# Gate product of the second block in seven block products instead of eight, with the block sums of its weights formed by transfers in DRAM

## The chip, the cores and the metric

One core of a Trainium2 chip runs the whole program in one launch. The metric is device time in microseconds (us). The kernel before took 2392.82 us (median of three runs, 2391.46 to 2393.68).

## The reference, cut to what matters

Two transformer-like blocks run one after the other on 512 tokens of width 2048, in fp32. The change touches only the end of the second block:

```python
def second_block(x, p, ...):
    ...
        merged = g_a * (o_a @ w_up_a[l]) + g_b * (o_b @ w_up_b[l])
        x = x + merged @ w_out[l]
        x = x + jax.nn.sigmoid(x @ w_ple_gate[l]) * (p[l] @ w_ple[l])
    return rms_norm_2(x, final_g)
```

The *gate product* is `x @ w_ple_gate`, a 512 x 2048 by 2048 x 2048 product. Each result passes a sigmoid, is multiplied by `p @ w_ple` (formed at the start of the kernel and kept in DRAM as `ple`), is added to `x`, and at last each token's row is normalised by its mean square and multiplied by `final_g`.

## The kernel before

**Precision.** TensorE multiplies fp32r tiles, which hold a rounded fp32. So each fp32 operand is split (`split`, L331) into a high part `hi`, a rounded copy made on ScalarE (`whi<-wraw`), and a low part `lo = raw - hi`, made on VectorE (`wlo<-wraw,whi`). `mm3` (L339) then issues three matmuls: hi by hi, hi by lo, lo by hi. Where the weight streams (as in the gate product), the first of the three needs the weight's `hi`, and the second its `lo`.

**Units.** All weight products are a list `spine` of `Unit`s (L237). A unit is one weight block: a DMA on SP's queue into a 4 KB-per-partition buffer (512 KB in all, `wraw`), its split into two more such buffers, and its matmuls. There are ten of these buffers (`NW`). A second pool of 78 buffers of 2 KB per partition (`NSLOT`) holds activations.

**Order.** The program is written out by hand in one order, and each engine and each queue runs its share in that order. While the matmuls of unit i are written, `ahead` (L148) writes DMAs up to unit i+3 (`LD = 4`) and splits up to unit i+2 (`LS = 3`) and no further, provided that a small time model (`Clock`, L147) does not have VectorE or ScalarE over 5 us ahead of TensorE. Unit i+3's split is thus written after everything that belongs to unit i. Side work (generators in `Sides`, L181) is put between matmuls by `pump`, one step at a time, as long as the model has VectorE and ScalarE at most 3 us ahead of TensorE.

**The last stages.** `w_in_2` (units 127 to 302 of the list), then `w_up_a_2`/`w_up_b_2` (32 units), then the `w_out_2` product (L2031, 32 units, *out2* below). Out2 makes the new x in 16 tiles of 128 channels x 512 tokens; each (L2012) is added, split into `x2h`, `x2l`, transposed by TensorE (`px2`) and stored to DRAM token by token (`x2t`).

**The gate product.** Five column groups (`GATES`: 512, 512, 512, 256, 256). The 128 x 128 tiles of x2 are the stationary operand, the weight streams. In the groups of 512, `panel_units` (L852) makes 8 units; a unit covers two of the 16 channel tiles and, for each of four token blocks b, issues 2 x 3 matmuls of 512 columns, 24 in all. In the unit that ends a group, each b's sum is followed by `after_gate` (L2065): tanh on ScalarE, two VectorE operations (`tgate<-tgate,plel` and `x<-tgate,x`), a square with row sum on ScalarE, and a VectorE product with `final_g`. The last group (`whole_units`, L878) holds all its weight and finishes token block after token block; `finish` (L2090) forms 1/sqrt on VectorE in small steps (`part`), scales the four column blocks on ScalarE and VectorE, and stores them.

Of the kernel before, what the change touches and what calls it, by code (L numbers as in the profile page):

```python
# [8 lines left out]
F32 = mybir.dt.float32  # L9
# [72 lines left out]
GATES = ((0, 512), (512, 512), (1024, 512), (1536, 256), (1792, 256))  # L82


def blocks():
# [4 lines left out]
    def cut(ks, c0, c1, n):  # L90
# [9 lines left out]
    gate = [b for i, (c0, n) in enumerate(GATES)  # L100
            for b in cut(rows(KT, (512 if i == len(GATES) - 1 else 1024) // n), c0, c0 + n, n)]
# [135 lines left out]
class Unit:  # L237
    def __init__(self, src, shape, mm, pre=None, hold=1, half=False):

        self.src, self.shape, self.mm, self.pre, self.hold, self.half = src, shape, mm, pre, hold, half  # L240
        self.raw = self.hi = self.lo = None


def emit(ctx, tc, I, out):
# [1171 lines left out]
    done = {"oa": [], "ob": [], "sg": []}  # L1416
# [579 lines left out]
    x2h, x2l = [None] * KT, [None] * KT  # L1996
    x2_d = dram("x2t", (128, TB, D))
    xl = {}

    def load_x1(m):  # L2000
        if m < KT:
            xl[m] = slot([128, 512], "x1l")
            dma("G", xl[m], x1_d[m])

    def out2_pre(m):
        def fn():
            if m == 0:
                load_x1(0)
            load_x1(m + 1)
        return fn  # L2010

    def after_o2(m):  # L2012
        def fn(ps):
            x = xl.pop(m)
            tt(x, ps, x, OP.add)
            x2h[m], x2l[m] = slot([128, 512], f"x2h{m}", F32R), slot([128, 512], f"x2l{m}", F32R)
            split(x, x2h[m], x2l[m])
            sides.spawn(x2_gen(m, x))
        return fn

    def x2_gen(m, x):
# [7 lines left out]
        dma("G", x2_d[:, :, m * 128:(m + 1) * 128], o)  # L2029

    for m in range(KT):  # L2031
        spine += ch_units("w_out_2", m * 128, 128, after_o2(m), out2_pre(m), KT, (mgh, mgl))


    ssq = cp.tile([128, TB, 8], F32, name="ssq")
    x3 = {}
    pl_ = {}

    def gate_load(i):
        if i >= len(GATES):  # L2040
            return
        c0, n = GATES[i]
        for b in range(TB):
            if c0 % 512 == 0:
                x3[b, c0 // 512] = slot([128, 512], "x3")
            p = slot([128, n], "plel")
            dma("G", p, ple_d[b][c0 // 512][:, c0 % 512:c0 % 512 + n])
            dma("G", x3[b, c0 // 512][:, c0 % 512:c0 % 512 + n], x2_d[:, b, c0:c0 + n])
            pl_[i, b] = p

    def gate_pre(i):
        def fn():
            if i == 0:
                sides.drain()
# [7 lines left out]
    last = len(GATES) - 1  # L2062
    part = {}

    def after_gate(i):  # L2065
        def fn(b, ps):
            c0, n = GATES[i]
            t = slot([128, n], "tgate")
            act(t, ps[:, :n], AF.Tanh, scale=0.5)
            x = x3[b, c0 // 512][:, c0 % 512:c0 % 512 + n]  # L2070
            fg = pl_["fg", c0 // 512][:, c0 % 512:c0 % 512 + n]
            stt(t, t, 1.0, pl_[i, b], OP.add, OP.mult)
            stt(x, t, 0.5, x, OP.mult, OP.add)
            if i < last:
                act(t, x, AF.Square, accum_out=ssq[:, b, i:i + 1])
                tt(x, x, fg, OP.mult)
                if i == last - 1:
                    sides.spawn(part_gen(b))
                return
            stt(t, x, 1.0, x, OP.mult, OP.mult, accum_out=ssq[:, b, i:i + 1])  # L2080
            sides.spawn(finish(b, x, fg))
        return fn
# [136 lines left out]
```

## Time and profile before

| | |
|---|---|
| median of three runs | 2392.82 us |
| the profiled execution | 2393.15 us, its span 2391.4 us |
| TensorE busy | 99% of the span |
| VectorE, ScalarE, GpSimd busy | 62%, 39%, 11% |
| mean DMA rate | 141 GB/s |

The profile names PE for TensorE's matmuls, PEld for its weight loads, DVE for VectorE, ACT for ScalarE, POOL for GpSimd and SP for SyncE, whose queue loads the weights. Times of the timeline are us from the start of the span. A matmul's row has its own duration, longer than the distance between starts since matmuls overlap. "[0.78 <-DVE x1l L283]" means that the engine stood idle for 0.78 us before the row and that the end of that VectorE operation released it.

### The profile page before, as it was taken

The page shows a single profiled execution, that of the slowest core. Times are in us where ns is not written, and L with a number is a line of the kernel's source. Part 1 is how long each engine was busy: PE and PEld are TensorE (multiplying, and loading weights), DVE is VectorE, ACT ScalarE, POOL GpSimd, SP SyncE. Part 2 cuts the span into 40 slices and gives each one's busy share as a digit, 9 for nine tenths or more (in the row PEclk, how much of TensorE's full clock was granted, in tenths as well). Part 3 has the DMA queues.
Part 4 walks back from the last instruction along what each step waited for, and adds up shares of the span by engine and source line. Part 5 has one row for each costly group of instructions (what it writes and reads, how often), then busy time and mean ns, then how long its engine had stood idle before and what let it go on. Part 6 is the DMA issues. An engine that isn't in the chain of part 4 may idle for free.

```text
span 2391.4 us, 31046 instructions
## 1 busy us (share of the span) xinstructions
PE 2360.1 (99%) x11587; PEld 1985.0 (83%) x11587; DVE 1478.4 (62%) x2816; ACT 929.6 (39%) x1724; POOL 251.1 (11%) x376
## 2 busy tenths in 40 slices
PE   7999999999999999999999999999999999999998
PEld 5778889888888988888888888888888888888887
DVE  6787988788865367558878437777233444333336
ACT  5423265655533343335444234544233222222223
POOL 0000030332212001000000000000012100111201
PEclk9999999999999999999999999999999999999999
DMA  9986732333355333222222232222345533444633
GB/s 334 351 272 241 257 129 71 124 124 101 111 181 175 92 108 132 90 92 89 93 86 96 93 97 89 93 85 89 124 164 175 202 105 109 140 141 145 219 103 118
DMA packets 115783, 336.98 MB, mean 141 GB/s; under 512 B 15326, under 2 KB 15620, under 8 KB 115632
## 3 DMA queue, kind: packets, MB, share of 16 engines
q1 hardware_dynamic: 92016, 260.83, 32.8%
q0 software_dynamic: 22752, 73.02, 9.1%
q8 instruction: 91, 1.49, 0.3%
q10 hardware_dynamic: 864, 1.14, 0.1%
q14 instruction: 60, 0.49, 0.1%
HBM read 297.18 MB, written 37.75 MB: 140 GB/s over the span
## 4 chain that ended last, share of the span: by engine, by line
PE 85%; issue 6%; DVE 5%; ACT 2%; DMA 1%; POOL 1%; SPq 0%; POOLq 0%; DVEq 0%; ACTq 0%
PE pch L320 45%; PE ppan L320 14%; PE pp L320 9%; PE po L320 6%; PE psc L320 3%; PE pO L320 3%; PE pPT L324 2%; PE pearly L320 1%; DVE wlo L283 1%; PE pple L320 1%; PE pmod L534 1%; ACT whi L314 0%; DVE cA L283 0%; PE pada L320 0%; DMA wraw<-in_w_in_dram 0%
## 5 line engine op out<-in xcount | busy, mean ns | idle before, releaser
L283 DVE TENSOR_TENSOR wlo<-wraw,whi 128x1024 fp32r<-128x1024 f32 (+5 forms) x401 | 468.0, 1169 | 210.1 <-ACT whi L314 204.9
L314 ACT ACTIVATE whi<-wraw 128x1024 fp32r<-128x1024 f32 (+5 forms) x403 | 399.4, 1003 | 326.1 <-PE pch L320 115.1
L320 PE MATMUL pch<-h2h,whi 128*128 128x512 f32 x1216 | 483.3, 397 | 0.0
L320 PE MATMUL pch<-h2h,wlo 128*128 128x512 f32 x1216 | 474.9, 391 | 0.0
L320 PE MATMUL pch<-h2l,whi 128*128 128x512 f32 x1216 | 474.6, 390 | 0.0
L320 PEld LDWEIGHTS pch<-h2h,wlo 128*128 128x128 f32 x1216 | 228.2, 188 | 48.6
L320 PEld LDWEIGHTS pch<-h2h,whi 128*128 128x128 f32 x1216 | 228.6, 188 | 41.1
L320 PEld LDWEIGHTS pch<-h2l,whi 128*128 128x128 f32 x1216 | 228.8, 188 | 40.8
L314 ACT ACTIVATE P<-psc,sm 128x512 f32<-128x512 f32 (+3 forms) x160 | 83.6, 526 | 134.1 <-DVE sm L306 103.9
L320 PE MATMUL pp<-hh,whi 128*128 128x512 f32 x320 | 126.0, 394 | 0.2 <-DVE acc L283 0.2
L320 PE MATMUL pp<-hh,wlo 128*128 128x512 f32 x320 | 124.7, 390 | 0.0
L320 PE MATMUL pp<-hl,whi 128*128 128x512 f32 x320 | 124.6, 389 | 0.0
L320 PE MATMUL ppan<-whi,x2h 128*128 128x512 f32 (+1 forms) x320 | 111.0, 347 | 0.0
L320 PE MATMUL ppan<-whi,x2l 128*128 128x512 f32 (+1 forms) x320 | 110.9, 347 | 0.0
L320 PE MATMUL ppan<-wlo,x2h 128*128 128x512 f32 (+1 forms) x320 | 110.9, 347 | 0.0
L320 PE MATMUL pch<-mgh,whi 128*128 128x512 f32 x256 | 101.1, 395 | 0.0
L320 PE MATMUL pch<-mgh,wlo 128*128 128x512 f32 x256 | 99.9, 390 | 0.0
L320 PE MATMUL pch<-mgl,whi 128*128 128x512 f32 x256 | 99.7, 389 | 0.0
L320 PE MATMUL pch<-oh,whi 128*128 128x512 f32 x256 | 99.6, 389 | 0.0
L320 PE MATMUL pch<-ol,whi 128*128 128x512 f32 x256 | 99.6, 389 | 0.0
L320 PE MATMUL pch<-oh,wlo 128*128 128x512 f32 x256 | 99.6, 389 | 0.0
L314 ACT ACTIVATE PTh<-pPT 128x512 fp32r<-128x512 f32 (+1 forms) x120 | 59.5, 528 | 91.1 <-PE pPT L324 88.7
(500 smaller groups left out, 4635.0 us busy)
## 6 DMA issues: line engine op xcount, KB each, us to landing
wraw<-in_w_in_dram SPq DMA_DIRECT2D x199, 512.0 KB, 3.5
wada<-in_w_mod_dram SPq DMA_DIRECT2D x128, 256.0 KB, 5.4
wraw<-in_w_out_dram SPq DMA_DIRECT2D x64, 512.0 KB, 3.5
wgate<-in_w_gate_dram SPq DMA_DIRECT2D x64, 256.0 KB, 4.9
wraw<-in_w_ple_gate_dram SPq DMA_DIRECT2D x28, 512.0 KB, 3.5
sg<-mg POOLq DMA_DIRECT2D x32, 256.0 KB, 2.5
wraw<-in_w_up_b_dram SPq DMA_DIRECT2D x16, 512.0 KB, 3.5
sgl<-sg POOLq DMA_DIRECT2D x32, 256.0 KB, 6.1
```

The source lines that it names most:

```text
L283: V.tensor_tensor(o, a, b, op=op)
L314: A.activation(o, a, fn, **k)
L320: T.matmul(o, l, r, start=start, stop=stop_)
L324: T.transpose(o, a, i)
L534: T.matmul(acc[32 * q:32 * q + 32, :], cc[:, k, :], w.rearrange("p s n -> p (s n)"), start=first, stop=last_)
```

## The change

The gate product is done in two pairs of 512-wide column blocks (p = 0, 1). Within a pair x is cut in four quarters (rows: tokens 0 to 255 and 256 to 511; columns: channels 0 to 1023 and 1024 to 2047) and the weight in four (1024 x 512 each). Seven products of a quarter-sized left form with a quarter-sized right form (Strassen's method in Winograd's version) take the place of eight. They run in the order 1, 7, 6, 2, 5, 3, 4.

- Left forms: `F[q, k]`, one 128 x 2 x 256 tile (hi and lo) for each product q and each of 8 channel tiles, 56 tiles. Those of products 1, 7, 6 are made beside out2 (`early_forms`), the others beside the first products of pair 0 (`late_forms`). Both pairs use them.
- Right forms: three products use blocks of the weight as they are; for the other four, sums of blocks are formed in DRAM by 64 POOL transfers of 512 KB, half of them copies and half accumulating (`wsums`), one after every second unit from unit 150 on.
- A unit is now two channel tiles by two token blocks j: 12 matmuls of 512 columns. A product has 4 units and a pair 28. `after_prod`, called for each j in a product's fourth unit, puts the products together; products 2, 5, 3 and 4 each complete a result and go through `gated` (tanh, two VectorE operations, square).
- The product with `final_g` is moved: for pair 0 into the start of products 7, 6 and 2 of pair 1, for pair 1 behind `gated`.
- The very last product holds its four units' weight and runs j = 0 whole and j = 1 in two halves of 256 columns; `finish` is called per token block as before.
- Out2's 16 tiles come in the order 0, 8, 1, 9, ... instead of 0, 1, 2, ...; x2h and x2l of whole tiles are no longer made.
- `thin`, a way to form a unit's low part by an accumulating DMA, is in the code but off (`THIN = False`): all low parts that were on VectorE stay there.

```diff
-GATES = ((0, 512), (512, 512), (1024, 512), (1536, 256), (1792, 256))
+THIN = False
+SUMS = 150
...
-    gate = [b for i, (c0, n) in enumerate(GATES)
-            for b in cut(rows(KT, (512 if i == len(GATES) - 1 else 1024) // n), c0, c0 + n, n)]
+    gate = cut(rows(KT, 2), 0, D, 512)
...
+    O2 = [m for k in range(8) for m in (k, k + 8)]
...
     def after_o2(m):
         def fn(ps):
-            x = xl.pop(m)
+            x = x2r[m] = xl.pop(m)
             tt(x, ps, x, OP.add)
-            x2h[m], x2l[m] = slot([128, 512], f"x2h{m}", F32R), slot([128, 512], f"x2l{m}", F32R)
-            split(x, x2h[m], x2l[m])
             sides.spawn(x2_gen(m, x))
+            if m >= 8:
+                sides.spawn(early_forms(m - 8))
...
+    def quarters(k):
+        a, c = x2r[k], x2r[k + 8]
+        return a[:, 0:256], c[:, 0:256], a[:, 256:512], c[:, 256:512]
+    def form(q, k, x):
+        t = slot([128, 2, 256], "F" + q, F32R)
+        act(t[:, 0], x, AF.Copy)
+        yield [t]
+        tt(t[:, 1], x, f(t[:, 0]), OP.subtract)
+        F[q, k] = t
+    def early_forms(k):
+        x11, _, x21, x22 = quarters(k)
+        yield [x22]
+        yield from form("1", k, x11)
+        s = slot([128, 2, 256], "fs")
+        tt(s[:, 0], x11, x21, OP.subtract)
+        tt(s[:, 1], s[:, 0], x22, OP.add)
+        yield [s]
+        yield from form("7", k, s[:, 0])
+        yield from form("6", k, s[:, 1])
+    def late_forms():
+        for k in range(8):
+            yield
+            yield from form("2", k, quarters(k)[1])
+        for k in range(8):
+            x11, x12, x21, x22 = quarters(k)
+            yield
+            s = slot([128, 2, 256], "fs")
+            tt(s[:, 0], x21, x22, OP.subtract)
+            yield [s]
+            yield from form("5", k, s[:, 0])
+            tt(s[:, 1], x12, x11, OP.subtract)
+            tt(s[:, 1], s[:, 1], s[:, 0], OP.add)
+            yield [s]
+            yield from form("3", k, s[:, 1])
+            x2r.pop(k)
+        for k in range(8):
+            yield
+            yield from form("4", k, x2r[k + 8][:, 256:512])
+            x2r.pop(k + 8)
...
+    PROD = ("1", "7", "6", "2", "5", "3", "4")
+    PAIRS = (0, 1)
...
+    def wsums():
+        for p in PAIRS:
+            for step in range(8):
+                for u in range(4):
+                    d = {n: ws_d[p, n, u].rearrange("p (k n) -> p k n", k=2) for n in ("x1", "x2", "x3", "y1")}
+                    o, a = ((d["x1"], wblock(p, 0, 0, u)), (d["y1"], wblock(p, 1, 1, u)), (d["x1"], wblock(p, 0, 1, u)),
+                            (d["y1"], wblock(p, 0, 1, u)), (d["x2"], d["x1"]), (d["x2"], wblock(p, 1, 1, u)),
+                            (d["x3"], d["x2"]), (d["x3"], wblock(p, 1, 0, u)))[step]
+                    if step in (2, 3, 5, 7):
+                        G.dma_start(o, a, accum_op=OP.add, max_dma_last_dim=4096)
+                        clock.dma("G", o, a)
+                    else:
+                        dma("G", o, a)
+                    yield
...
+    def gated(b, c, src, s=slice(0, 512), end=False):
+        x = x3[b, c][:, s]
+        t = slot([128, 512], "tgate")[:, s]
+        act(t, src, AF.Tanh, scale=0.5)
+        stt(t, t, 1.0, pl_[b, c][:, s], OP.add, OP.mult)
+        stt(x, t, 0.5, x, OP.mult, OP.add)
+        o = ssq[:, b, c:c + 1]
+        if end:
+            o = small("sqe")[:, 0:1]
+            stt(t, x, 1.0, x, OP.mult, OP.mult, accum_out=o)
+        else:
+            act(t, x, AF.Square, accum_out=o)
+        return o
+    def scaled(b, c):
+        x = x3[b, c]
+        tt(x, x, pl_["fg", c], OP.mult)
...
+    def after_prod(p, q, j):
+        c = 2 * p
+        ps = acc[q, j] if q == "7" else acc.pop((q, j))
+        if q == "1":
+            t = tmp["1", j] = slot([128, 512], "q1")
+            act(t, ps, AF.Copy)
+        elif q == "6":
+            w = tmp["w", j] = slot([128, 512], "wq")
+            tt(w, ps, tmp["1", j], OP.subtract)
+        elif q == "2":
+            t = tmp.pop(("1", j))
+            tt(t, ps, t, OP.add)
+            gated(j, c, t)
+        elif q == "5":
+            e, t, w, p7 = slot([128, 512], "eq"), slot([128, 512], "c22"), tmp["w", j], acc.pop(("7", j))
+            tmp["e", j] = e
+            tt(e, ps, w, OP.add)
+            tt(t, e, p7, OP.subtract)
+            tt(w, p7, w, OP.subtract)
+            gated(2 + j, c + 1, t)
+        elif q == "3":
+            t = tmp.pop(("e", j))
+            tt(t, ps, t, OP.add)
+            gated(j, c + 1, t)
+        elif q == "4":
+            t = tmp.pop(("w", j))
+            tt(t, ps, t, OP.add)
+            gated(2 + j, c, t)
+        if p == 1:
+            if q in "253":
+                b, cc_ = {"2": (j, c), "5": (2 + j, c + 1), "3": (j, c + 1)}[q]
+                scaled(b, cc_)
+            if q == "3":
+                sides.spawn(finish(j, ()))
+            if q == "5":
+                sides.spawn(part_gen(2 + j))
...
+            if p == 0:
+                sides.until(lambda: (q, 2 * u + 1) in F)
+            if u:
+                return
+            if p == 0 and q == "1":
+                for _ in sums_:
+                    pass
+                sides.spawn(late_forms())
+            if p == 1 and q == "1":
                 for c in range(4):
-                    t = slot([128, 512], "fg")
+                    t = pl_["fg", c] = slot([128, 512], "fg")
                     dma("G", t, bcast(I["final_g_2"], 512, c * 512))
-                    pl_["fg", c] = t
-            gate_load(i)
+            if p == 1 and q in "762":
+                for b, c in {"7": ((0, 0), (1, 0)), "6": ((2, 1), (3, 1), (0, 1)), "2": ((1, 1), (2, 0), (3, 0))}[q]:
+                    scaled(b, c)
+            if q in OUT:
+                sides.until(lambda: done["x2"] == KT)
+                b, c = OUT[q]
+                for j in range(2):
+                    gate_load(b + j, 2 * p + c)
...
+    def prod_units(p, q):
+        last_ = p == 1 and q == "4"
+        held = {}
+        def mk(u):
+            def mmf(hi, lo):
+                if last_:
+                    held[u] = (hi, lo)
+                    if u == 3:
+                        yield from last_product(held)
+                    return
+                for j in range(2):
+                    if u == 0:
+                        acc[q, j] = bank("pg" + q)
+                    ps = acc[q, j]
+                    t = slice(j * 128, (j + 1) * 128)
+                    for kk in range(2):
+                        w = F[q, 2 * u + kk]
+                        mm3(ps, w[:, 0, t], w[:, 1, t], hi[:, kk, :], lo[:, kk, :], u == 0 and kk == 0,
+                            u == 3 and kk == 1)
+                        yield
+                    if u == 3:
+                        after_prod(p, q, j)
+                        yield
+                if p == 1:
+                    for kk in range(2):
+                        F.pop((q, 2 * u + kk))
+            return Unit(wsrc(p, q, u), (2, 512), mmf, pre=prod_pre(p, q, u),
+                        hold=(4 if u == 3 else 0) if last_ else 1, thin=THIN and p == 0 and u % 2 == 1)
+        return [mk(u) for u in range(4)]
...
+    def last_product(ws):
+        for j in range(2):
+            t = slice(j * 128, (j + 1) * 128)
+            sums = []
+            for s in (slice(0, 512),) if j == 0 else (slice(0, 256), slice(256, 512)):
+                ps = bank("pg4")[:, s]
+                for k in range(8):
+                    hi, lo = ws[k // 2]
+                    w = F["4", k]
+                    mm3(ps, w[:, 0, t], w[:, 1, t], hi[:, k % 2, s], lo[:, k % 2, s], k == 0, k == 7)
+                    yield
+                x = tmp["w", j][:, s]
+                tt(x, ps, x, OP.add)
+                sums.append(gated(2 + j, 2, x, s, s.stop == 512))
+            sides.spawn(finish(2 + j, sums))
+            yield
...
+    for p in PAIRS:
+        for q in PROD:
+            spine += prod_units(p, q)
...
+        if i >= SUMS and i % 2 == 0:
+            next(sums_, None)
```

## Rows read from the trace of the kernel before

**Rows 1.** The page's first part: busy time, share of the span, instructions.
```profile
PE 2360.1 (99%) x11587; PEld 1985.0 (83%) x11587; DVE 1478.4 (62%) x2816; ACT 929.6 (39%) x1724; POOL 251.1 (11%) x376
```

**Rows 2.** Stretches: length; busy by engine; granted TensorE clock, DMA share, GB/s.
```profile
2028.00:2202.60 174.60, 173.82 (x798) 143.54 (x797) 58.23 (x61) 45.72 (x61) 17.75 (x28) 1.00 0.44 134
...
2202.60:2379.20 176.60, 176.60 (x962) 154.15 (x961) 79.36 (x142) 54.67 (x93) 25.56 (x48) 1.00 0.44 150
...
2384.60:2391.40 6.80, 0.00 (x0) 0.00 (x0) 0.00 (x0) 0.06 (x1) 0.54 (x1) 0.50 0.42 154
```

**Rows 3.** Timeline of TensorE: start us, us, line, tiles, idle before and its releaser.
```profile
2202.19 0.66 PE L324 MATMUL px<-cst,x1l 128*128 128x128 f32 x4 [0.78 <-DVE x1l L283]
...
2205.21 0.39 PE L320 MATMUL ppan<-whi,x2l 128*128 128x512 f32 x1
...
2214.51 0.39 PE L320 MATMUL ppan<-wlo,x2h 128*128 128x512 f32 x1
...
2375.39 0.28 PE L320 MATMUL ppan<-whi,x2h 128*128 128x256 f32 x1
...
2377.55 0.28 PE L320 MATMUL ppan<-whi,x2h 128*128 128x256 f32 x1
```

**Rows 4.** Timeline of ScalarE around the end of the first column group.
```profile
2242.36 0.60 ACT L314 ACTIVATE tgate<-ppan 128x512 f32<-128x512 f32 x1 [4.31 <-PE ppan L320]
2244.44 0.63 ACT L314 ACTIVATE tgate<-x 128x512 f32<-128x512 f32 x1 [1.48 <-DVE x L302]
...
2253.50 2.94 ACT L314 ACTIVATE whi<-wraw 128x1024 fp32r<-128x1024 f32 x3
```

**Rows 5.** The same stretch of VectorE.
```profile
2242.99 0.69 DVE L302 SCALAR_TENSOR_TENSOR tgate<-tgate,plel 128x512 f32<-128x512 f32 x1 [3.68 <-ACT tgate L314]
2243.72 0.69 DVE L302 SCALAR_TENSOR_TENSOR x<-tgate,x 128x512 f32<-128x512 f32 x1
2245.19 0.69 DVE L283 TENSOR_TENSOR x<-x,fg 128x512 f32<-128x512 f32 x1 [0.79 <-ACT tgate L314]
2245.80 0.69 DVE L302 SCALAR_TENSOR_TENSOR tgate<-tgate,plel 128x512 f32<-128x512 f32 x1
...
2254.58 1.23 DVE L283 TENSOR_TENSOR wlo<-wraw,whi 128x1024 fp32r<-128x1024 f32 x1 [0.26 <-ACT whi L314]
```

**Rows 6.** Groups from 1900 us on: shapes and count, busy us, mean ns, idle before.
```profile
L314 ACT ACTIVATE whi<-wraw 128x1024 fp32r<-128x1024 f32 x79 | 81.3, 1048 | 63.1 <-PE ppan L320 49.8 <-DMA wraw<-in_w_ple_gate_dram 10.2 <-ACT whi L314 1.9
...
L283 DVE TENSOR_TENSOR x1l<-pch,x1l 128x512 f32<-128x512 f32 x16 | 11.1, 691 | 100.7 <-PE pch L320 100.7
...
L314 ACT ACTIVATE x2h<-x1l 128x512 fp32r<-128x512 f32 x16 | 10.1, 631 | 132.8 <-DVE x1l L283 132.8
...
L283 DVE TENSOR_TENSOR x<-x,fg 128x256 f32<-128x256 f32 x4 | 1.7, 426 | 2.3 <-ACT tgate L314 2.3
```

**Rows 7.** Timeline of the last token block's end on VectorE and POOL.
```profile
2381.98 1.31 DVE L302 SCALAR_TENSOR_TENSOR part<-part 128x1 f32<-128x1 f32 x6
2383.33 0.48 DVE L302 SCALAR_TENSOR_TENSOR x<-x,part,fg 128x256 f32<-128x256 f32 x1
...
2384.76 0.54 POOL L328 DMA_DIRECT2D out_dram<-x  x1 [5.22 <-DVE x L292]
```

**Rows 8.** DMA issues from 1351 to 1551 us: KB each, median us to landing.
```profile
wraw<-in_w_in_dram SPq DMA_DIRECT2D x28, 512.0 KB, 3.5
```

**Rows 9.** DMA issues from 2202 to 2255 us.
```profile
wraw<-in_w_ple_gate_dram SPq DMA_DIRECT2D x9, 512.0 KB, 4.4
plel<-ple POOLq DMA_DIRECT2D x12, 256.0 KB, 6.9
```

**Rows 10.** Timeline of TensorE: the kernel's first matmuls, and a wait in `w_in_2`.
```profile
11.64 0.63 PE L320 MATMUL pple<-whi,pTh 128*128 128x512 f32 x1
...
15.05 0.63 PE L320 MATMUL pple<-whi,pTl 128*128 128x512 f32 x1
...
914.01 0.39 PE L320 MATMUL psv<-wT,vnh 128*128 128x256 f32 x1 [1.59 <-DVE wT L283]
```

More of the change, by code (lines that the diff above doesn't have):

```diff
@@ L237, with __init__ @@
 class Unit:
-    def __init__(self, src, shape, mm, pre=None, hold=1, half=False):
+    def __init__(self, src, shape, mm, pre=None, hold=1, half=False, thin=False):
         self.src, self.shape, self.mm, self.pre, self.hold, self.half = src, shape, mm, pre, hold, half
+        self.thin = thin
         self.raw = self.hi = self.lo = None
@@ L2029, in x2_gen @@
         dma("G", x2_d[:, :, m * 128:(m + 1) * 128], o)
[L2031 to L2049, printed above, removed]
@@ new lines, in emit, with wblock @@
+    for n, m in enumerate(O2):
+        spine += ch_units("w_out_2", m * 128, 128, after_o2(m), out2_pre(n), KT, (mgh, mgl))
+    PROD = ("1", "7", "6", "2", "5", "3", "4")
+    PAIRS = (0, 1)
+    ws_d = {(p, n, u): dram(f"ws{p}{n}{u}", (128, 1024)) for p in PAIRS for n in ("x1", "x2", "x3", "y1") for u in range(4)}
+    def wblock(p, i, j, u):
+        k, c = 8 * i + 2 * u, (2 * p + j) * 512
+        return block("w_ple_gate_2", k, k + 2, (c, c + 512))
+    def wsums():
[12 more added lines that the diff above has]
+                    yield
@@ new lines, in wsrc, with gate_load @@
+    def wsrc(p, q, u):
+        if q in "123":
+            return wblock(p, *{"1": (0, 0), "2": (1, 0), "3": (1, 1)}[q], u)
+        return ws_d[p, {"7": "y1", "6": "x2", "5": "x1", "4": "x3"}[q], u].rearrange("p (k n) -> p k n", k=2)
+    ssq = cp.tile([128, TB, 4], F32, name="ssq")
+    x3, pl_, acc, tmp, part = {}, {}, {}, {}, {}
+    def gate_load(b, c):
+        x3[b, c] = slot([128, 512], "x3")
+        pl_[b, c] = slot([128, 512], "plel")
+        dma("G", pl_[b, c], ple_d[b][c])
+        dma("G", x3[b, c], x2_d[:, b, c * 512:(c + 1) * 512])
@@ L2086, in part_gen, with finish @@
         p = part[b] = small("part")
-        reduce(p[:, 0:1], ssq[:, b, :last], OP.add)
+        tt(p[:, 0:1], ssq[:, b, 0:1], ssq[:, b, 1:2], OP.add)
+        tt(p[:, 0:1], p[:, 0:1], ssq[:, b, 3:4], OP.add)
         ts(p[:, 0:1], p[:, 0:1], 1.0 / D, EPS, OP.mult, OP.add)
-    def finish(b, x, fg):
+    def finish(b, sums):
         yield
-        ms = part[b]
-        stt(ms[:, 0:1], ssq[:, b, last:last + 1], 1.0 / D, ms[:, 0:1], OP.mult, OP.add)
+        if sums:
+            ms = part[b]
+            for o in sums:
+                stt(ms[:, 0:1], o, 1.0 / D, ms[:, 0:1], OP.mult, OP.add)
+        else:
+            ms = part[b] = small("part")
+            reduce(ms[:, 0:1], ssq[:, b, :], OP.add)
+            ts(ms[:, 0:1], ms[:, 0:1], 1.0 / D, EPS, OP.mult, OP.add)
         r = rsqrt1(ms)
         yield
-        stt(x, x, r, fg, OP.mult, OP.mult)
-        for c in range(4):
-            y = x3[b, c] if c < 3 else x3[b, c][:, :GATES[last][0] - 1536]
-            if c < 2:
+        for n, c in enumerate((2, 3, 1, 0)):
+            y = x3[b, c]
+            if sums and c == 2:
+                stt(y, y, r, pl_["fg", c], OP.mult, OP.mult)
+            elif n < 3:
                 act(y, y, AF.Identity, scale=r)
@@ L2102, in finish @@
                 ts(y, y, r, None, OP.mult)
[L2103 removed]
+            dma("QAQG"[n], out[0, b * 128:(b + 1) * 128, c * 512:(c + 1) * 512], y)
     def rsqrt1(ms):
@@ L2114, in rsqrt1 @@
         return y
-    for i, (c0, n) in enumerate(GATES):
-        spine += panel_units("w_ple_gate_2", ((c0, c0 + n),), x2h, x2l, KT, (512 if i == last else 1024) // n, after_gate(i),
-                             gate_pre(i), i == last)
+    for p in PAIRS:
+        for q in PROD:
+            spine += prod_units(p, q)
     issued = {"dma": 0, "split": 0, "live": 0, "i": 0}
@@ L2141, in split_next @@
             gtt(u.lo, u.raw, f(u.hi), OP.subtract)
+        elif u.thin:
+            act(u.hi, u.raw, AF.Copy)
+            act(u.lo, f(u.hi), AF.Copy, scale=-1.0)
+            G.dma_start(u.lo, u.raw, accum_op=OP.add, max_dma_last_dim=4096)
+            clock.dma("G", u.lo, u.raw)
         else:
```

43 lines of the change are left out of this document (12 added, 31 removed).

## The prediction

> **What bounds the kernel now.** I read the page's first part, then the stretches, then TensorE's timeline across the last two stages, then what VectorE and ScalarE do where a column group of the gate product ends. TensorE is busy for 99% of the span [rows 1], and in the gate stage all the time: 176.60 of 176.60 us, with VectorE at 79 and ScalarE at 55 us beside it [rows 2]. So the time of this stage is matmul columns. The timeline gives the price of one: from 2205.21 to 2214.51 lie 41 starts, 0.2269 us per matmul of 512 columns, and from 2375.39 to 2377.55 lie 18 starts, 0.120 us per matmul of 256 columns [rows 3].
>
> The reader should then see how little slack holds this up. Behind the last matmuls of a group stand four chains (tanh, two VectorE operations, square), and the weight split of the third unit ahead is written behind them. The group's last unit starts at 2202.60 + 7 x 5.445 = 2240.72 (a unit is 24 x 0.2269 = 5.445 us); its first sum is taken at 2242.36; ScalarE makes the next `hi` at 2253.50 [rows 4] and VectorE its `lo` from 2254.58 to 2255.81 [rows 5]. Two units were split before the stage began and eight more up to here (counted on ScalarE's timeline), so this is unit 10, whose matmuls start at 2202.60 + 10 x 5.445 = 2257.05. It comes 1.2 us early, and TensorE sees nothing of it.
>
> **The change part by part.** *Matmuls.* Before: 3 groups x 8 units x 24 = 576 of 512 columns (130.7 us) and 384 of 256 (46.1 us), together 176.8 us. After: 14 products x 48 = 672, of which the last 24 become 48 of 256: 648 x 0.2269 + 48 x 0.120 = 152.8 us. That removes **24.0 us**. At the border the transposes of the last x2 tile stood ahead of the first gate matmul and cost an idle 0.78 us [rows 3]; they no longer have to come first: **0.9 us** with the restart. Gain 24.9 us.
>
> *Splits.* 56 units of 1024 elements per partition are split (57344 in all) in place of 36 units with 32768. One takes 1.05 us on ScalarE [rows 6] and 1.23 us on VectorE [rows 5]. A unit now lasts 12 x 0.2269 = 2.72 us instead of 5.445, so the rate is carried (1.23 of 2.72), but the lead of three units shrinks from 16.3 to 8.2 us.
>
> *Chains at the ends of products.* This is the main cost, worked out from the start (t = 0) of a product's fourth unit. The first sum is ready 1.36 us later (six matmuls), taken 0.2 us after that as at 2242.36, so 1.56. Product 2, 3 or 4 of pair 0: add 0.69 us [rows 6] to 2.25; tanh, now from SBUF, 0.63 us (the like of `x2h` [rows 6]), 2.29 to 2.92; two dependent VectorE operations, 0.73 us from start to start [rows 5], 2.95 to 4.37; square 4.40 to 5.03. The second j's add starts 0.61 us after the first j's last operation did, as at 2245.19 to 2245.80 [rows 5]: 4.29; its tanh waits for the square: 5.03 to 5.66; 5.69 to 7.11; square to 7.77. Only now comes the split of unit 3 ahead: `hi` to 8.82, `lo` to 10.08. That unit starts at 3 x 2.72 = 8.17 and needs `lo` with its second matmul at 8.40. It is **1.7 us late**, where before it was 1.2 us early. Product 5 has two more VectorE operations per j on the chain (0.69 each, one of them under the tanh): **3.1 us**. In pair 1 the product with `final_g` follows each square, which VectorE waits for (0.75 us from the square's start, 2244.44 to 2245.19 [rows 4, 5]): 3.1 us for product 2, **4.6** for product 5. Products 1, 7 and 6 end with a copy or one add and cost nothing. Pair 0: 1.7 + 3.1 + 1.7 + 1.7 = 8.2 us. Pair 1 up to product 5: 7.7 us.
>
> *Left forms.* 56 tiles of 128 x 256 replace 16 splits of 512. The late ones are 56 VectorE operations of 0.43 us [rows 6], 24 us inside pair 0. VectorE's sum there: 28 x 1.23 + 30 x 0.69 + 24 = 79 us, plus some 5 us of waiting for tanh, against 7 x 10.9 = 76 us of matmuls. The side work is held back when the model's lead is over 3 us, but a chain can begin up to that late. Bounds: nothing, and the whole overhang of 84 less 76 = 8 us. I take **3 us**, since three of the four chains of pair 0 meet late forms and the early ones lie in out2, where VectorE is busy 58 of 175 us [rows 2].
>
> *The end.* Product 3 of pair 1 ends like product 2 (square at 8.6), and behind it stand the splits of the last product's third and fourth unit, since no matmul separates them: `lo` of the third at 11.5. The last product needs it after 12 matmuls, at 2.72 + 2.72 + 0.23 = 5.68: **5.9 us** late. From there VectorE has the fourth `lo` (to 12.7), two `finish` chains (six of their small steps alone take 1.31 us [rows 7]; about 2.4 us each), the j = 0 chain (2.8), the first half's (1.8) and the third `finish` (3.1): to 25.2, while the matmuls end at 19.9. The last half's chain starts **5.3 us** late. It also has an add more than before and a wider last product: 0.7 us. Together 11.9 us.
>
> *Transfers of the sums.* 64 POOL transfers of 512 KB between units 150 and 278, one per two units (10.9 us). No row shows a copy within DRAM or an accumulating one. The nearest is a 512 KB load, landing after 3.5 us [rows 8]; with three passes over memory 10.5 us, still inside the spacing. From below it is nothing; a gain is excluded, since nothing is taken off a queue. From above, one late load of POOL's per stage, some 5 us. I take 0. The weights' own queue then moves 512 KB per 2.72 us, 193 GB/s, and the gate loads beside it. Under such loads a weight landed after 4.4 us [rows 9]; the buffers let its DMA start four units (10.9 us) ahead, and 4.4 + 1.05 + 1.23 fits.
>
> *Sum.* 2393.15 - 24.9 + 8.2 + 3 + 7.7 + 11.9 = **2399 us**. The profiled execution lies 0.33 us above the median, which is within what I can resolve; 2399 stands for both.
>
> **Clock.** In the trace waits of 0.78 and 1.59 us left the matmuls at full pace [rows 3, 10], and the granted clock fell to half (1.2 GHz) only at the very end, over 5 us behind the last matmul [rows 2]. The gap of about 5 us in the last product (5.45 to `hi` at 10.3) is near that. The Trainium skill ("TensorE: Matmul & The Clock Gate", section "HAM oscillation — how this bites in real kernels") says that idle gaps between bursts of matmuls put the engine back to the low clock, so that every burst starts cold; by it all seven gaps above could count and the sum would be rival 3's upper time; by the rows at most the last does, which leaves 2399 or adds that rival's single step.
>
> **Rivals.**
> 1. *The splits stay ahead, and the matmuls' gain arrives.* Place: the third unit behind each of the seven product ends. It decides at 8.40 us after a fourth unit's start: a `lo` that is there by then costs nothing. For it: VectorE rows overlap by 0.08 us where they are independent, and the miss in pair 0 is only 1.7 us. Against: the order of the code and the 1.2 us of rows 4 and 5, which shrink with the unit. With no wait at all and a late tail of 6 us: 2393.15 - 24.9 + 6 = 2374; with half of the waits (15): 2384.
> 2. *Gain and waits cancel.* The chains cost what I count, but forms and the last `finish` chains are hidden: 2393.15 - 24.9 + 8.2 + 7.7 + 5.9 + 0.7 = 2391.
> 3. *The low clock.* A cold stretch at the first matmuls ran at 0.426 us per matmul (11.64 to 15.05, eight starts [rows 10]), until 15.48: some 14 matmuls, 2.8 us lost. Once, in the last product: 2402. Seven times: 2419.
> 4. *The weights' DMA becomes the bound.* Each product that ends a result draws 1 MB of `ple` and x2 on POOL's queue; such loads landed after 6.9 us [rows 9]. If they hold back the weights by 1.4 us per unit for six units: 2407. Against: these loads are 8 MB in 153 us, and POOL's queue can issue them ahead as buffers come free.
>
> **How the numbers follow.** This kernel's measurement can't tell less than 0.2% (4.8 us) from no change: "same" is 2388.0 to 2397.6. Forecast 0.35 (its own range 2394 to 2405; 0.07 of it is "same"), rival 1 0.26 (0.01 of it "same"), rival 2 0.20, rival 3 0.11, rival 4 0.08. Faster 0.25, same 0.28, slower 0.47. For 8 in 10 the range runs from 2376 to 2409: it leaves out the lowest third of rival 1 and the repeated cold clock.
>
> **What would show it.** Right: in the gate stage TensorE's waits are put down to `wlo`, about seven of them of 1.5 to 6 us, the longest ahead of the last product; VectorE is busy for over 80% there; 672 + 24 matmuls in place of 960, at 0.227 us where nothing waits; the last block's chain starts some 5 us behind the last matmul. The clock term is right if the granted clock stays 1.00 until the last product. Wrong: TensorE busy without a gap through the product ends, or waits that DMA ends, or a slower `w_in_2` stage, from which the sums' transfers were not as free as I take them.

## The result: slower by 1%, with the low clock as the largest miss

The changed kernel takes **2416.51 us** (median of four runs, 2413.85 to 2417.46) against 2392.82: a ratio of 1.0098, with a 95% interval of 1.008 to 1.0115. The forecast was 2399 with a range to 2409. The sign was right; the size was not.

The profile of the changed kernel is of the 2413.85 us execution (its span 2412.0). First the page's busy line, then the stretches (length, busy by engine, granted TensorE clock, DMA share, GB/s): the gate stage, two of its pieces at the low clock, and what follows the last matmul.

```profile
PE 2349.8 (97%) x11323; PEld 1965.0 (81%) x11323; DVE 1543.5 (64%) x2928; ACT 971.2 (40%) x1785; POOL 290.5 (12%) x432
```
```profile
2200.20:2394.20 194.00, 168.43 (x702) 134.99 (x700) 138.84 (x218) 90.65 (x140) 21.11 (x39) 0.93 0.60 201
2258.60:2262.00 3.40, 2.96 (x7) 2.38 (x8) 2.92 (x5) 1.76 (x3) 0.00 (x0) 0.50 0.05 19
...
2381.40:2388.20 6.80, 5.13 (x11) 3.76 (x12) 5.85 (x20) 3.28 (x6) 0.40 (x1) 0.50 0.00 0
2394.20:2412.00 17.80, 0.24 (x3) 0.04 (x1) 8.98 (x35) 4.12 (x8) 1.08 (x2) 0.62 0.34 128
```

Against [rows 2] the stage went from 176.8 to 194.0 us, although it holds 264 matmuls fewer ([rows 1] against the first line here), and its granted clock from 1.00 to 0.93. At the unchanged pace the stage's matmuls would take 152.8 us. The 41.2 us on top divide in two. Each distance of over 0.6 us between the starts of neighbouring matmuls, less one matmul's 0.227, is a wait: fifteen of them, 29.0 us. Of the other 12.2 us, 11.1 are matmuls at the low clock and about 1.1 short gaps at the full one. The granted clock was 0.50 (the level of 1.2 GHz) in six stretches, 27.3 us in all. Waits of TensorE by what ended them (total, times, longest):

```profile
PE pg L322 <- ACT whi L316: 14.6, 6, 4.7
...
PE pg L322 <- DVE wlo L285: 4.2, 6, 0.8
PE pg L322 <- DVE F L285: 4.0, 1, 4.0
PE pg L322 <- ACT F L316: 2.7, 2, 2.0
```

So 18.8 us wait for the halves of a weight and 6.7 for a left form. (The profile counts idle time from the end of the matmul before, so these waits come to 25.5 us and not to 29.0.) The chain behind product 2 of pair 0 shows both, in ScalarE's timeline and then VectorE's:

```profile
2244.81 0.63 ACT L316 ACTIVATE tgate<-q 128x512 f32<-128x512 f32 x1 [3.02 <-DVE q L285]
...
2249.65 0.63 ACT L316 ACTIVATE tgate<-x 128x512 f32<-128x512 f32 x1 [1.49 <-DVE x L304]
...
2250.28 1.99 ACT L316 ACTIVATE whi<-wraw 128x1024 fp32r<-128x1024 f32 x2
```
```profile
2242.96 0.42 DVE L285 TENSOR_TENSOR F<-fs,F 128x256 fp32r<-128x256 f32 x1
2243.30 0.42 DVE L285 TENSOR_TENSOR fs<-x1l 128x256 f32<-128x256 f32 x1
2243.75 0.42 DVE L285 TENSOR_TENSOR fs<-fs 128x256 f32<-128x256 f32 x1
2244.09 0.68 DVE L285 TENSOR_TENSOR q<-pg,q 128x512 f32<-128x512 f32 x1
...
2251.35 3.58 DVE L285 TENSOR_TENSOR wlo<-wraw,whi 128x1024 fp32r<-128x1024 f32 x3 [1.73 <-ACT whi L316]
```

The fourth unit starts at 2241.58. The prediction has the first add 1.56 us later (2243.14), `hi` from 7.77 (2249.35) and `lo` done at 10.08 (2251.66). Three operations of the late forms stand ahead of the add, and all three marks come 0.9 us late (2244.09, 2250.28, 2251.35 + 1.23 = 2252.58): the chain's length is as worked out.

TensorE's timeline, behind product 5 and then at product 4 of pair 0, shows what a wait brings with it:

```profile
2267.79 0.39 PE L322 MATMUL pg<-whi,F 128*128 128x512 f32 x1
2270.36 0.50 PE L322 MATMUL pg<-whi,F 128*128 128x512 f32 x1 [2.18 <-ACT whi L316]
2271.61 0.50 PE L322 MATMUL pg<-wlo,F 128*128 128x512 f32 x1 [0.76 <-DVE wlo L285]
...
2273.00 1.05 PE L322 MATMUL pg<-whi,F 128*128 128x512 f32 x2
2273.85 0.63 PE L322 MATMUL pg<-wlo,F 128*128 128x512 f32 x1
2274.28 1.05 PE L322 MATMUL pg<-whi,F 128*128 128x512 f32 x2
...
2276.29 0.62 PE L322 MATMUL pg<-whi,F 128*128 128x512 f32 x2
...
2286.59 1.22 PE L322 MATMUL pg<-whi,F 128*128 128x512 f32 x2 [4.02 <-DVE F L285]
```

After 2.18 and 0.76 us of waiting, three matmuls take 1.28 us (2273.00 to 2274.28, 0.427 each) in place of 0.68, until 2275.6. Waits of 1.47 and 0.76 us (2249.5 to 2252.6) and of 0.58 and 0.76 us (2301.8 to 2304.0) left the pace alone; the first low stretch came after 0.69 and 1.98 us more, at 2258.6. No fixed length of wait comes out of the runs: in the kernel with splits one unit further ahead (below), two waits of 0.82 and 0.75 us, at 2325.0 and 2326.3, were followed by 3.4 us at a granted clock of 0.50.

### The profile page after: what moved, and what is told of

Its sections match the earlier page's. It is cut to its first block, busy times and chain, and to the rows that moved or that the text cites. A ratio compares the mean times of both kernels' runs of the same rounds, so it can differ in the third digit from the quotient of the medians.

```text
span 2412.0 us, 30852 instructions
## 1 busy us (share of the span) xinstructions
PE 2349.8 (97%) x11323; PEld 1965.0 (81%) x11323; DVE 1543.5 (64%) x2928; ACT 971.2 (40%) x1785; POOL 290.5 (12%) x432
## 4 chain that ended last, share of the span: by engine, by line
PE 53%; issue 6%; DVE 3%; ACT 1%; POOL 1%; DMA 0%; POOLq 0%; DVEq 0%; ACTq 0%
PE pch L322 45%; PE pO L322 2%; PE psc L322 2%; PE pPT L326 1%; PE pg L322 1%; DVE wlo L285 1%; ACT whi L316 0%; DVE cA L285 0%; PE pcs L322 0%; PE px L326 0%; DMA w1r<-in_cmp_w_v_dram 0%; DVE vx L304 0%; POOL x L330 0%; POOL plel L330 0%; PE psv L322 0%
## 5 line engine op out<-in xcount | busy, mean ns | idle before, releaser
L285 DVE TENSOR_TENSOR wlo<-wraw,whi 128x1024 fp32r<-128x1024 f32 (+5 forms) x421 | 498.0, 1184 | 190.6 <-ACT whi L316 188.1
L316 ACT ACTIVATE whi<-wraw 128x1024 fp32r<-128x1024 f32 (+5 forms) x423 | 424.2, 1013 | 321.8 <-PE pch L322 120.4
L322 PE MATMUL pg<-whi,F 128*128 128x512 f32 (+1 forms) x464 | 149.4, 403 | 21.3 <-ACT whi L316 14.6
L322 PEld LDWEIGHTS pg<-whi,F 128*128 128x128 f32 x464 | 91.4, 200 | 43.4 <-ACT whi L316 17.2
L322 PE MATMUL pg<-wlo,F 128*128 128x512 f32 (+1 forms) x232 | 93.8, 404 | 4.2 <-DVE wlo L285 4.2
```

The source lines that it names most:

```text
L285: V.tensor_tensor(o, a, b, op=op)
L316: A.activation(o, a, fn, **k)
L322: T.matmul(o, l, r, start=start, stop=stop_)
```

## The experiments

The theory: the time is lost to the order on VectorE and ScalarE (weight halves and late forms queued behind the chains), and to the low clock that these waits bring. Rivals: the transfers in DRAM and the weights' DMA; VectorE's load as such, whatever its order; a low clock without a cost of its own. Each ratio below is to the kernel before, on the same chip.

**The low clock, first attempt.** `warm` is called ahead of and between the three matmuls that wait.
```diff
+    def warm(w, n):
+        if n:
+            ps = bank("warm")
+            g = F[w].rearrange("p a b -> p (a b)")
+            for _ in range(n):
+                T.matmul(ps, g[:, 0:128], g, start=True, stop=True)
```


> The changed kernel with extra matmuls (their sums are read by nobody) put where TensorE waits at the product ends, 111 of 512 columns in all, each group a little shorter than the wait that the changed kernel's trace shows there, so that TensorE is not idle in them. Theory (waits for splits behind the chains, 29 us, and on top the half clock that follows them, 27.3 us at half pace, worth 11.9 us): the waits stay, filled; the clock stays at full; about 12 us less than the changed kernel, near 2404. Rival (the clock is only a mark of the waits and costs nothing by itself, or falls whatever TensorE does): the time stays at 2416 or grows. Rival (the extra matmuls lengthen the stage): up to 25 us more.

Measured: 2420.75, ratio 1.0118 (1.0102 to 1.0134). Inconclusive: the added matmuls read the form of the matmul they precede, and waited for it themselves:

```profile
PE warm L2190 <- DVE F L285: 6.9, 3, 4.2
```

Low clock in the stage fell to 13.7 us only. Where the fill fitted (product 3 of pair 0, 5 and 4 of pair 1), the product got 1.5, 1.5 and 2.0 us shorter; products 5 and 4 of pair 0 and 3 of pair 1 got 3.0, 4.0 and 1.6 us longer.

**Splits one unit further ahead.**
```diff
-        fetch(i + LD)
+        ls, ld = (LS + 1, LD + 1) if i >= GATE0 - 1 else (LS, LD)
+        fetch(i + ld)
```
(and `ls` for `LS` in the test below it)

> The changed kernel with one number changed in the gate stage: weights are fetched and split one unit further ahead (splits up to unit i+3 instead of i+2), so that the unit that stood behind the chains is split before them. Theory: the unit behind the chain is now needed 2.72 us later. The waits after products 2, 3 and 4 of pair 0 go, after product 5 and after product 2 of pair 1 about 0.4 us is left, after product 5 of pair 1 1.9 us, in the last product 4.5 us; the waits for late left forms (some 6 us) stay; the clock falls less often. Some 20 us less than the changed kernel, near 2395. Rival (weights' DMA or the forms bound the stage): less than 5 us gained.

Measured: 2439.11, ratio 1.0192 (1.0174 to 1.021). The expectation fell. In pair 0 the late forms now come later than the weights did:

```profile
PE pg L322 <- ACT F L316: 18.2, 4, 10.5
PE pg L322 <- ACT whi L316: 17.1, 6, 5.8
```

So part of the lateness moved to the forms. That is only part of it: pair 1, which makes no forms, takes 112.5 us in place of 97.8, which is 14.7 of the 26.0 us that the gate stage grows. Its longest waits (6.0, 4.9 and 4.9 us) are still for a weight's `hi`. The queue that loads the weights shows a second cause, which the expectation didn't have. Its waits for the end of a low-part split, first in the changed kernel and then here:

```profile
SPq L330 <- DVE wlo L285: 23.6, 5, 8.5
```
```profile
SPq L330 <- DVE wlo L285: 98.8, 34, 9.9
```

ScalarE's splits then wait 56.5 us for weights to land, where it was 19.0. The longer lead is written, but the weights come too late for it; that the ten buffers are too few for it is likely and was not tested.

**No sums in DRAM.**
```diff
+        return wblock(p, *{"7": (0, 1), "6": (0, 0), "5": (1, 1), "4": (1, 0)}[q], u)
...
-    sums_ = wsums()
+    sums_ = iter(())
```


> The changed kernel without the 64 transfers of the block sums; products 7, 6, 5 and 4 read single blocks of the weight in place of the sums, so this leaves out part of the computation. Theory: the transfers are free; within 2 us of the changed kernel. Rival (they slow the stages that they run beside, or the memory): 5 to 20 us less than the changed kernel, with the gain before 2200 us of the span.

Measured: 2415.09, ratio 1.0095 (1.0079 to 1.0111), as the changed kernel. The sums cost nothing that the runs can tell. The changed kernel's trace shows why (issues from 1351 to 1551 us, KB each, median us to landing): the weights beside them land in 3.5 us, as in [rows 8].

```profile
wraw<-in_w_in_dram SPq DMA_DIRECT2D x31, 512.0 KB, 3.5
...
ws1x<-ws1x POOLq DMA_DIRECT2D x4, 512.0 KB, 4.0
ws1y<-in_w_ple_gate_dram POOLq DMA_DIRECT2D x2, 512.0 KB, 5.8
ws1x<-in_w_ple_gate_dram POOLq DMA_DIRECT2D x2, 512.0 KB, 5.5
```

**No late forms.**
```diff
+            if p == 0 and q == "2" and u == 0:
+                for q2, q1 in (("2", "1"), ("5", "7"), ("3", "6"), ("4", "1")):
+                    for k in range(8):
+                        F[q2, k] = F[q1, k]
...
-                sides.spawn(late_forms())
```


> The changed kernel without the 32 late left forms; products 2, 5, 3 and 4 use the tiles of products 1, 7, 6 and 1 in their place, so this leaves out part of the computation. It takes 56 VectorE operations (24 us) out of pair 0. Theory: the waits after product 2 and in product 4 of pair 0 shrink from 5.6 and 4.2 us to the 1.7 us each that the chain alone gives, with less time at the half clock; pair 1 stays as it is; 8 to 12 us less than the changed kernel. Rival (the forms are the main cost, VectorE being over-subscribed in pair 0): pair 0 runs without waits, 18 to 20 us less. Rival (forms are hidden): no change.

Measured: 2411.13, ratio 1.0074 (1.0058 to 1.0089): 5.4 us less than the changed kernel, where 8 to 12 were expected. Product 4 of pair 0 takes 12.73 us instead of 18.05. No wait for `F` is left, but 16.6 us for `whi` are, and the clock is low for 34.1 us. One wait grew: behind product 2 of pair 0 it is 4.7 us, where the chain alone was to give 1.7 and the changed kernel has 2.7. There VectorE had a split ahead of the add, and this split waited for a weight's transfer (ScalarE stood idle for 1.39 us until it landed at 2244.53), so the add began at 2246.76 instead of 2243.77. The forms are a part, by this run the smaller one; the run prices them only roughly.

**No chains.**
```diff
     def gated(b, c, src, s=slice(0, 512), end=False):
+        if not end and src.shape[-1] == 512:
+            V.memset(ssq[:, b, c:c + 1], 1.0)
+            return ssq[:, b, c:c + 1]
```


> The changed kernel without the chain behind each result of 512 columns (tanh, two VectorE operations, square; left out of the computation, the sums of the products stay). Theory (splits behind the chains are the cost): the waits after results go, those for late left forms shrink or go, the clock stays at full; the gate stage takes 153 to 160 us instead of 194, and 35 to 40 us less than the changed kernel, near 2378. Rival (VectorE's total work or the forms bound the stage): a gain of 10 to 20 us only, with waits for forms left. Rival (the weights' DMA): waits that DMA ends take their place.

Measured: 2385.98, ratio 0.9973 (0.9962 to 0.9983). Behind the very first product, which shares TensorE with the border's transposes, twelve products take 10.88 to 10.99 us, which is their pace (48 x 0.2267), with all late forms in place; the last one takes 23.70, still waiting 8.0 us for `whi` and `wlo`. For this reason the stage takes 165.7 us instead of the expected 153 to 160, and the kernel is 30.5 us below the changed one instead of 35 to 40. These last waits are not of the chains left out here: the scales of `finish` stand ahead of one split on ScalarE (2347.03 to 2349.42), and the last weight's transfer is issued only at 2350.05, behind output stores on SP's queue that waited for such a scale. Without the chains the forms cost nothing; without the forms the chains still cost most of it.

**The same chains, in another order.** `later` does the work of `gated`, but as side work, step by step, so that weight splits are written between its steps.
```diff
+    def later(b, c, src, fin=None, also=None):
+        yield [src]
+        x = x3[b, c]
+        t = slot([128, 512], "tgate")
+        act(t, src, AF.Tanh, scale=0.5)
+        yield [t]
+        stt(t, t, 1.0, pl_[b, c], OP.add, OP.mult)
+        stt(x, t, 0.5, x, OP.mult, OP.add)
+        yield [x]
+        act(t, x, AF.Square, accum_out=ssq[:, b, c:c + 1])
+        if also:
+            yield [t]
+            scaled(b, c)
...
-            gated(j, c, t)
+            sides.spawn(later(j, c, t, None, p == 1))
```


> The changed kernel with the chain behind each result (tanh, two VectorE operations, square, product with final_g) taken out of the product's end and given to the side work, one step at a time, so that splits are written between its steps; nothing is left out. Theory (order on VectorE and ScalarE, not their work): most of the waits behind products go, 15 to 30 us less than the changed kernel, 2387 to 2402. Rival (VectorE's work in pair 0, 79 us and more of 76, is the bound): waits move to the late left forms, which are now written even later, and the time stays within 8 us.

Measured: **2381.36** (2381.15 to 2384.46), ratio **0.9959** (0.9945 to 0.9973): the fastest kernel of the study, 5.6 us below the expected range. VectorE works as much (144 us from the first gate matmul to the end, 148 in the changed kernel); the order is new. The stretches of its gate stage and of its tail, and VectorE behind product 2 of pair 0:

```profile
2201.10:2357.30 156.20, 154.79 (x702) 127.23 (x700) 131.11 (x197) 86.73 (x134) 20.03 (x37) 1.00 0.70 238
2357.30:2379.50 22.20, 0.02 (x1) 0.00 (x0) 13.12 (x56) 8.12 (x14) 2.18 (x4) 0.61 0.50 189
```
```profile
2245.22 1.28 DVE L285 TENSOR_TENSOR q<-pg,q 128x512 f32<-128x512 f32 x2
2246.42 1.22 DVE L285 TENSOR_TENSOR wlo<-wraw,whi 128x1024 fp32r<-128x1024 f32 x1
...
2248.22 0.68 DVE L304 SCALAR_TENSOR_TENSOR tgate<-tgate,plel 128x512 f32<-128x512 f32 x1
```

The low part now goes ahead of the chain, not behind it. The stage's matmuls take 156.0 us with one wait of over 0.6 us left, and the granted clock is 1.00 throughout. This is 20.8 us less than before; 10.3 of it are given back behind the start of the last matmul, where 22.4 us remain in place of 12.2.

**The sums of the forms on GpSimd as well.**
```diff
-            tt(s[:, 0], x21, x22, OP.subtract)
+            gtt(s[:, 0], x21, x22, OP.subtract)
+            gtt(s[:, 1], x12, x11, OP.subtract)
+            gtt(s[:, 1], s[:, 1], s[:, 0], OP.add)
...
```


> As the kernel with the chains as side work, and in addition the 24 differences and sums of the late left forms for products 5 and 3 on GpSimd instead of VectorE (10 us less VectorE work in pair 0). Theory of order alone: the same as that kernel within 3 us. Rival (VectorE's work in pair 0): 5 to 12 us less than that kernel.

Measured: 2384.06, ratio 0.9966 (0.9953 to 0.9979), not faster than the deferred chains alone: products 7 and 6 of pair 0 take 13.16 and 12.35 us. It lies within the 3 us of the theory, but it is no test of VectorE's load, since what stayed on VectorE got slower: from 2202 to 2240 us one `F<-x1l,F` takes 1043 ns on the mean (421 with the deferred chains alone) and one `wlo<-wraw,whi` 1530 (1223); the last section says more of this. That VectorE's load as such is not the bound follows from the deferred chains alone, where the same operations run without the waits.

**Low parts by accumulating DMA.** `THIN = True`, for every second unit of pair 0.

> The changed kernel with every second unit of pair 0 forming its low part by an accumulating transfer (14 of the 28 low parts, 17 us of VectorE's work in pair 0, at the price of a second ScalarE copy each). Theory of order: the other 14 splits still stand behind the chains, and a low part by transfer needs a DMA's landing, 2.5 us or more, behind the same chain; the waits of pair 0 stay or grow, between 5 us less and 10 us more than the changed kernel. Rival (VectorE's work is the bound in pair 0): 10 to 15 us less.

Measured: 2448.89, ratio 1.0233 (1.0216 to 1.025): 32.4 us above the changed kernel, where at most 10 were expected. Taking VectorE work away makes it slower where the replacement has a longer latency: nine such transfers of pair 0 landed 5.6 us (median) after their issue, where a low part on VectorE takes 1.22. TensorE's wait for them:

```profile
PE pg L322 <- DMA wlo<-wraw: 24.2, 9, 5.3
```

**The low clock, second attempt.** As the first, but `warm` reads a form of product 1, which has long been there, and the counts are nearer to the waits. It holds 113 added matmuls, not the 98 of the expectation.
```diff
+            g = keepF.setdefault(0, F.get(("1", 0))).rearrange("p a b -> p (a b)")
```


> The changed kernel with 98 added 512-column matmuls into a bank that nothing reads, in the waits of the gate stage alone, this time on a form and a rhs tile that have long been there, so that the added matmuls themselves wait for nothing; counts fitted to the waits of the changed kernel's trace (at 0.227 us each). Theory: 27 of the gate stage's us ran at 1.2 GHz after the waits, and this costs about 12 us beside the waits themselves; with the waits filled the granted clock stays at 1.0 there, the low-clock time falls from 27 to under 12 us, and the time falls by 5 to 12 us, to 2405 to 2412. Rival: the low clock is no cost of its own, since a faster TensorE only arrives earlier at the next late half of the weights: the waits grow by what the pace gives, and the time stays within 3 us of the changed kernel's 2416.

Measured: 2411.12, ratio 1.0074 (1.0061 to 1.0087), 5.4 us below the changed kernel and within the expected range.

```profile
2202.60:2390.20 187.60, 182.20 (x815) 147.66 (x813) 136.88 (x215) 90.48 (x140) 21.18 (x39) 1.00 0.61 205
```

No low clock is left in the stage. Its matmuls go from 194.0 to 187.3 us, so 6.7 of the 11.1 us come back; 2.0 of them are given back behind the last matmul. The rest turns into waiting: added matmuls (113 x 0.227 = 25.7), waits (6.0) and small gaps (2.8) make 34.5 us where waits and small gaps were 30.1. The likely reason is that a TensorE at full pace reaches the next late half sooner; that some added matmuls ran past the end of the wait that they fill isn't excluded. The rival without any cost falls; so does the full cost.

**VectorE's backlog at the end.** Two kernels built on the one with the deferred chains, both aimed at its tail. The first edit stands in `later`, the second in `finish`, where it chooses which scales ScalarE takes. In the expectations e6 is the kernel with the deferred chains, e7 the one with the forms' sums on GpSimd as well, e10 the first of the two here.
```diff
-            scaled(b, c)
+            gtt(x, x, pl_["fg", c], OP.mult)
...
-            elif n < 3:
+            elif n < 3 or not sums:
```


> The kernel with the deferred chains (e6), with work of VectorE's last 40 us moved: pair 1's scaling by final_g of each tile goes to GpSimd (4 of 512 columns a pair half), and all final scales of the two last row groups go to ScalarE. If VectorE's backlog sets the end (VectorE busy without a pause from 2333 to 2373, 22.3 us behind the last matmul), the tail falls by the moved work, some 4 to 6 us, and the time to 2375 to 2378. Rival: the order of the drain (the partial sums and finish stand behind it in the list of side work) sets the end; then within 2 us of e6's 2381.

The second has this too, `thin` for every second unit of products 5, 3 and 4 of pair 1, and there:
```diff
-            G.dma_start(u.lo, u.raw, accum_op=OP.add, max_dma_last_dim=4096)
+            gtt(u.lo, u.raw, f(u.hi), OP.subtract)
```


> As e10, and besides the low part of every second unit of pair 1's products q5, q3 and q4 on GpSimd (ScalarE copies the negative, an accumulating transfer is replaced by GpSimd's subtraction). If VectorE's backlog sets the end, the tail falls by another 3 to 4 us (6 low parts of 0.7 us), to 2371 to 2375. Rival: GpSimd's slower subtraction makes the low part late for its matmuls, as the late forms' sums on GpSimd did in e7 (products up to 2.3 us over pace): then waits of 1 to 3 us in q5, q3 or q4 eat it, and the time is at or above e10's.

Measured: 2387.18, ratio 0.9975 (0.9964 to 0.9985), and 2391.80, ratio 0.9994 (0.9985 to 1.0003). Theory and rival of the first both miss: it isn't within 2 us of 2381 but 5.8 above, and its last matmul comes 2.9 us later than in the kernel it is built on. The second bears out its rival: 4.6 us above the first, with TensorE waiting 2.0 us for a low part of GpSimd's and 1.7 us for one of VectorE's. (Its expectation prices a low part at 0.7 us; a row gives 1.22.) In the first, VectorE did less and took longer for it. Groups from 2330 to 2362 us (count, busy, mean ns of one), VectorE with the deferred chains alone, then VectorE and GpSimd in the first of the two kernels:

```profile
L285 DVE TENSOR_TENSOR wlo<-wraw,whi 128x1024 fp32r<-128x1024 f32 x9 | 10.9, 1217 | 0.0
L304 DVE SCALAR_TENSOR_TENSOR x<-tgate,x 128x512 f32<-128x512 f32 x5 | 3.5, 692 | 0.2
```
```profile
L285 DVE TENSOR_TENSOR wlo<-wraw,whi 128x1024 fp32r<-128x1024 f32 x9 | 14.8, 1669 | 0.3
L304 DVE SCALAR_TENSOR_TENSOR x<-tgate,x 128x512 f32<-128x512 f32 x5 | 4.5, 909 | 0.2
```
```profile
L289 POOL TENSOR_TENSOR x<-x,fg 128x512 f32<-128x512 f32 x6 | 11.3, 1886 | 56.9 <-ACT tgate L316 56.8
```

Six products on GpSimd save VectorE 6 x 0.68 = 4.1 us; nine low parts lose 9 x 0.452 = 4.1 us to it, five `x<-tgate,x` another 1.1, and ScalarE's longer list of final scales ends the run. What could shorten the tail stays open.

## Why the prediction was wrong, point by point

- *Matmuls.* Right: a product without a wait takes 10.88 us, 48 x 0.2267. The first gate matmul starts at 2200.29 instead of 2202.60; the prediction had 0.9 us of this. Over the kernels of the study that start lies anywhere from 2200.3 to 2205.0, so the rest can't be told from the scatter.
- *Chains.* Right where they can be told. The waits beyond pace (from start to start) against the prediction: behind product 2 of pair 0, 2.7 us (1.7); product 5, 3.4 (3.1); product 4, 1.8 (1.7); in pair 1 product 2, 3.2 (3.1), product 5, 4.9 (4.6), and in the last product 5.9 (5.9). The excess behind product 2 of pair 0 is the forms' (below); the chain of product 3 of pair 0 stays hidden, since the next wait for a form comes ahead of it.
- *Left forms.* Too low: two waits inside product 5 of pair 0 cost 3.0 us by themselves, 0.9 us more stands in the wait behind product 2, and the second unit of product 4 waits 4.2 us for its form where the chain of product 3 was to cost 1.7. Together 6.4 us in place of 3. With the chain terms this makes waits of 29.0 us where 24.8 were forecast: 4.2 of the miss.
- *The end.* Right: the tail behind the last matmul grew by 5.6 us (12.2 to 17.8); 5.3 + 0.7 were forecast.
- *Sums and weights' DMA.* Right: nothing, as the kernel without the sums shows; rival 4 did not occur, since no wait of TensorE in the changed kernel's gate stage is put down to a DMA.
- *Clock.* **This step failed**: "by the rows at most the last does, which leaves 2399". The granted clock fell to half six times, not at most once, and 11.1 us of slow matmuls are the largest part of the miss. Of the 14.9 us between 2399 and the profiled 2413.85, the waits beyond forecast make 4.2, the slow matmuls 11.1 and short gaps 1.1; the earlier start takes 1.4 off, which leaves 15.0. The rows with waits of 0.78 and 1.59 us at full pace were carried over to waits of 2 to 6 us that no row showed. Each of the six low stretches came with a wait of about 2 us or more (1.98 the shortest); two of these waits were for left forms, which the prediction had too low. Rival 3's upper time, 2419, was the right mechanism at nearly the right count, at a mean of 1.8 us each instead of 2.8 (which counted 14 cold matmuls where the timeline holds 12), and its chance of 0.11 was too small. What a full clock would give back is less than 11.1 us: with the waits filled it was 5.4 us of the time, and the 2411 us left still lie above the range.
- *The rule on the clock.* By the Trainium skill ("TensorE: Matmul & The Clock Gate", section "HAM oscillation — how this bites in real kernels"), idle gaps between bursts put TensorE back to the low clock. The prediction weighed this and set it aside. The trace agrees in kind, with six low stretches and 27.3 us, but not for every gap: the waits of 1.47 and 0.76 us and of 0.58 and 0.76 us brought none.
- *Signs.* The waits for weights came as foretold, but more of them are put down to `whi` (14.6 us) than to `wlo` (4.2), and VectorE was busy for 72% of the stage, not for over 80%.
- *Rival 1* (2374 to 2384) is what the deferred chains turn the change into: 2381.36, by almost no wait and a tail of 10.3 us more instead of its 6. It was wrong for this code, as its "against" said: the order decides.

## What to carry to other kernels

When a change shortens the consumer's unit, the lead of its producers in time shrinks by the same factor; look at what stands in their queues at the end of each block, and put long chains of dependent steps behind or between the next operands' preparation, not ahead of it. Price a wait of TensorE that no row has shown with the low clock behind it as well: here 29 us of waits brought 11 us of slow matmuls, of which about half came back in the time when the waits were filled. Ask of work that is moved to a quieter engine or a DMA what its latency is and whom it shares operand reads with.

## What the runs showed of the hardware

A VectorE operation with both inputs in SBUF stood still while GpSimd worked on tiles. In the last kernel above, with low parts on GpSimd, VectorE and then GpSimd:

```profile
2335.56 0.69 DVE L285 TENSOR_TENSOR c<-eq,pg 128x512 f32<-128x512 f32 x1
...
2347.75 1.23 DVE L285 TENSOR_TENSOR part<-ssq 128x1 f32<-128x1 f32 x1
2349.02 2.31 DVE L285 TENSOR_TENSOR part<-part,ssq 128x1 f32<-128x1 f32 x1
2351.36 0.15 DVE L296 TENSOR_SCALAR part<-part 128x1 f32<-128x1 f32 x1
2351.43 0.68 DVE L285 TENSOR_TENSOR eq<-pg,eq 128x512 f32<-128x512 f32 x1
```
```profile
2335.66 2.41 POOL L289 TENSOR_TENSOR wlo<-wraw,whi 128x1024 fp32r<-128x1024 f32 x1
...
2346.71 2.25 POOL L289 TENSOR_TENSOR x<-x,fg 128x512 f32<-128x512 f32 x1
2348.93 2.38 POOL L289 TENSOR_TENSOR wlo<-wraw,whi 128x1024 fp32r<-128x1024 f32 x1
```

Two sums of 128 x 1 elements, 0.15 to 0.16 us elsewhere, last until GpSimd's operation of that moment ends (2348.98 and 2351.3); an operation with one input in PSUM (`c<-eq,pg`, 0.69 us) keeps its time beside GpSimd's low part of 2335.66. The Trainium skill says the same ("SBUF — State Buffer", section "SBUF: two separate sides": the port pair shared by the two engines is locked for a whole instruction), and the trace agrees.
